# Low parts of attention keys padded with zeros to 128 rows, in a three-block kernel whose first loads and first block are also put in another order

## The chip, the cores and the metric

One Trainium2 chip, one core. The metric is device time in microseconds (us) of one execution of the whole program; a kernel's time is the median of several runs. The core has TensorE (PE in the profile, its weight loads apart as PEld), VectorE (DVE), ScalarE (ACT), GpSimd (POOL) and SyncE (SP), which here issues transfers alone. Each engine runs its own list of instructions in order; it waits where an instruction needs a result of another engine.

## The reference

Three blocks run one behind the other on one sequence `x` of 512 positions and 1024 features, all in fp32:

```
x = first_block(x, c, ctx, ...)    # three branches (below), gated and summed, then a SwiGLU FFN
x = second_block(x, ...)           # 2 layers: FFN, hybrid attention mixer, FFN
x = third_block(x, c_3, ...)       # RG-LRU and attention side by side

# first_block: h = modulate(rms_norm(x), shift, scale), and of p = h @ w_in
o  = gla_bidir(q, k, v, gates)     # gated linear attention, chunks of 64, both directions, 4 heads
y_a = (norm(o) * silu(r)) @ w_o_gla
hc = depthwise_conv(c1 * sigmoid(c2), 31 taps)
y_b = silu(layer_norm(hc)) @ w_o_conv
y_c = (su * spatial_mix(layer_norm(sv))) @ w_o_sgu
y  = (gate0 * y_a + gate1 * y_b + gate2 * y_c) @ w_out

# second_block, mixer: 8 heads of 64 with a forget gate, 4 differential heads with two maps of 64 each
s = q @ k.T * scale + cum_q - cum_k     # causal, softmax, @ v
a = softmax(s1) - lam * softmax(s2)     # differential heads
# third_block: 8 heads of 64, which for 512 positions is plain causal attention
```

The shift and scale of each block are `silu(c) @ w_ada + b_ada`.

## The kernel before

**Products.** Features lie on partitions: `x` is 8 tiles of 128x512. A large product of fp32 operands is made of three matmuls on operands split into a high and a low part of fp32r (`mm3`): high times high, high times low, low times high. Weights stream through SP in 542 chunks of 128x1024 into three buffers `wraw`; ACT casts a chunk's high part (`whi`), and DVE subtracts it to make the low part (`wlo`; of odd chunks POOL does, in the attention stretches). A chunk feeds 24 of these main matmuls, which is also what one output tile of 128x512 takes of 1024 inputs (a unit below).

**Order.** Everything else (norms, gated linear attention, convolution, attention) is background work, written as Python generators. Behind each `mm3` the builder steps them (`tick`), and a generator goes on when the builder's own clock (`Clock`, with a price per instruction from `cost_pe`, `cost_act`, `cost_dve`, `cost_pool`) says that its operands are there and that enough tiles are free (`sync`, `room`, `wait`). What comes out is a fixed list of instructions for each engine. Nothing is reordered on the chip, so the prices shape the order of every engine. There are 78 blocks of 128x512 for intermediates (`b`) and 8 PSUM banks (`bk`). Where blocks run out, the builder lets the main matmuls stand and steps the background alone (`need`, `idle`). Convolution taps are a filler that is put in between on DVE.

**Attention.** `stack` takes a tile that holds the transposed queries or keys of two heads (64 rows each) and makes operands of 128 rows. For queries, operand e holds the high part of head e in its own 64 rows and the low part in the other 64. For keys, operand e holds the high part in both halves, and one more tile holds the low parts of both heads. `attn_scores` makes a block of 128 queries against up to 512 keys of two matmuls: 128 rows (both parts of the queries with the keys' high part), and then 64 rows (queries' high part, keys' low part):

```python
k.nc.tensor.matmul(b[:, o:o + n], lhsT=q[e].r[:, c], rhs=kk[e].r[:, 0:n], start=True, stop=False)
k.nc.tensor.matmul(b[:, o:o + n], lhsT=q[e].r[rows, c], rhs=kk[2].r[rows, 0:n], start=False, stop=True)
```

Each head (or map) has four such pairs, with 256, 256, 384 and 512 keys. There are 16 heads or maps in each layer of block 2 (layer 0 at some 1650 to 1830 us of the trace, layer 1 at 2660 to 2850) and 8 in block 3 (some 3340 to 3450). That makes 160 pairs, and 20 stacks of keys.

**Block 1's middle.** `ORDER_1` sets the order of units: `r` (8 gate units of the linear attention), `g` (8 units of branch gates for each of three branches), `p` (8 output products for each branch), `a` (wait until the linear attention is done), `v` and `s` (third branch). Branch 0 is the linear attention, branch 1 the convolution. In the trace the first `r` begins at 271.4 us, the first product (of branch 1) at 506.2, the first of branch 0 at 564.2, and `v` at 622.2.

**Start.** `Ada1` makes shift and scale: SP loads pieces of `w_ada` in four parts of 8 tiles; part 0 is multiplied on PE (`rows`), the others on DVE (`step`, then `sums` on PE and `finish`). Part q serves tiles 2q and 2q+1 of the first loop. `warm` issues fp32 matmuls of a zeroed tile whose results nothing reads. `prepare` makes tile m of the normalized and modulated input.

Of the kernel before, what the change touches and what calls it, by code (L numbers as in the profile page):

```python
# [18 lines left out]
S = 512  # L19
SC = 256  # L20
KT = 8
# [156 lines left out]
def width(ap):  # L178
    n = 1
    for d in tuple(ap.shape)[1:]:  # L180
        n *= d
    return n
# [41 lines left out]
def cost_dve(op, out, a, kw):  # L224
    n = width(out)
    if op == "reciprocal":
        return 0.07 + 6.4e-3 * n
    if op in ("tensor_scalar", "memset"):
        return max(0.2, 0.1 + 0.7e-3 * n)
    return max(0.2, 0.08 + 1.05e-3 * n)  # L230


def cost_pool(op, out, a, kw):
    return 0.06 + (1.0e-3 if op == "memset" else 2.3e-3) * width(out)


class Engine:
# [532 lines left out]
def stack(k, t, keys):  # L770


    nc = k.nc
    yield from k.sync()
    yield from k.room(4)
    out = [k.rblk(), k.rblk()]
    low = k.rblk() if keys else None
    own = [slice(0, 64), slice(64, 128)]
    for e in range(2):
        nc.scalar.copy(out[e].r[own[e]], t.f[own[e]])  # L780
    if keys:
        for e in range(2):
            nc.scalar.copy(out[e].r[own[1 - e]], t.f[own[e]])
    yield from k.sync()
    for e in range(2):
        lo = (low.r if keys else out[e].r)[own[e] if keys else own[1 - e]]
        nc.gpsimd.tensor_sub(lo, t.f[own[e]], out[e].f[own[e]])
    k.free(t)
    if keys:
        out.append(low)  # L790
    return out


def attn_scores(k, q, kk, e, part):
    b = k.bank()
    rows = slice(64 * e, 64 * e + 64)
    for qb, o in part:
        n, c = max((qb + 1) * P, 256), slice(qb * P, qb * P + P)
        k.nc.tensor.matmul(b[:, o:o + n], lhsT=q[e].r[:, c], rhs=kk[e].r[:, 0:n], start=True, stop=False)
        k.nc.tensor.matmul(b[:, o:o + n], lhsT=q[e].r[rows, c], rhs=kk[2].r[rows, 0:n], start=False, stop=True)  # L800
    return b


# [222 lines left out]
class Diff:  # L1026
# [3 lines left out]
    o = None  # L1030
# [834 lines left out]
def some(kind, ms, b=None):  # L1865
    return [(kind, m, b) for m in ms]


def between(b, ahead):

    o = []
    for m in range(KT):
        o += some("p", [m], b)
        if m + ahead < KT:
# [1 line left out]
    return o  # L1876


ORDER_1 = (some("r", range(KT)) + some("g", range(6), 1) + some("g", range(6), 0) + between(1, 6) + some("a", [0])
           + between(0, 6) + some("v", range(2)) + some("s", range(KT)) + some("g", range(6), 2) + between(2, 6))  # L1880


def plan1():
# [75 lines left out]
class Ada1:  # L1959
# [20 lines left out]
    def rows(self, q):  # L1980

        k, nc = self.k, self.k.nc
        b, row = k.bank(), k.blk()
        for t in range(KT):
            nc.tensor.matmul(b[0:2], lhsT=self.sc[:, t, :], rhs=self.ws[q][t].f, start=t == 0, stop=t == KT - 1)
        nc.scalar.copy(row.f[0:2], b[0:2])
        k.unbank(b)
        b = k.bank()
        for i in range(4):
            nc.tensor.transpose(b[:, 2 * i:2 * i + 2], row.f[0:2, i * P:i * P + P], k.ident[0:2, 0:2])  # L1990
        for c in range(2):
            self.finish(q, c, b[:, c:8:2])
        k.unbank(b)
        k.free(row, self.ws.pop(q))

    def step(self, q, c, t, acc):
        ve, w, s = self.k.nc.vector, self.ws[q][t].f, self.sc[:, t, c:c + 1]
# [91 lines left out]
def gla_dir(k, st, h, s, res):  # L2089
    nc = k.nc  # L2090
    b = yield from k.gbank()
    c0 = s * 512 + h * P
    nc.tensor.matmul(b, lhsT=st["aup"][c0 // 512].r[0:96, c0 % 512:c0 % 512 + P], rhs=st["adn"].r[0:96],
                     start=True, stop=True)
# [43 lines left out]
                         start=True, stop=True)  # L2138
    pairs = lambda ap: ap.rearrange("p (b c t) -> p b c t", c=2, t=64)
    chunk = dec.rearrange("p (b c) -> p b c", c=2)  # L2140
    nc.gpsimd.tensor_mul(both, chunk[:, :, 0], chunk[:, :, 1])
    f, l = pairs(kd.f)[:, :, s], pairs(qe.f)[:, :, 1 - s]
    nc.gpsimd.tensor_mul(f, f, chunk[:, :, 1 - s:2 - s].to_broadcast([P, 4, 64]))
    nc.gpsimd.tensor_mul(l, l, chunk[:, :, s:s + 1].to_broadcast([P, 4, 64]))
# [284 lines left out]
def block1(k, x, nxt):  # L2429
    nc = k.nc  # L2430
    w = "w_in"
    st = dict(q={}, k={}, v={}, r={}, o={}, ck={}, cv={}, s0=[k.blk() for _ in range(4)], cdone=0, hdone=0,
              conv={}, hc={}, yb={}, z={}, sv={})
    for m in range(KT):
        x.append(k.blk())
        nc.sync.dma_start(x[m].f, k.a["x"][:, m, :])
    ada = Ada1(k)
    ada.load(0)
    k.w_start()
    ada.load(1)  # L2440
    warm(k, 7)
    k.clk.t = k.clk.c["dve"] = k.clk.c["act"] = 6.0
    acc = sumsq(k, [x[m].f for m in range(KT)], S, nc.vector)
    lt, ly = rms_cols(k, acc.f, S, EPS1)
    ada.rows(0)
    bcb = bc_rows(k, ly)
    hx = []

# [7 lines left out]
        k.free(x[m])  # L2456

    prepare(0)
    k.w_ensure(1)
    k.w_finish(1)  # L2460
    prepare(1)
    ada.load(2)
    cols = k.bank()
# [4 lines left out]
    for m in range(KT):  # L2468
        q = m // 2 + 1
        if m % 2 == 0 and q < 4:  # L2470
            k.fresh()
            for t in range(KT):
                ada.step(q, 0, t, gacc)
            summed = k.clk.t
        for n, c0 in enumerate(first_units()):
            k.main_mm3(fb[n], k.wnext(w, 0, m, c0), (hx[m][0].r, hx[m][1].r), m == 0, m == KT - 1)
            if m % 2 == 1 and n == 1 and q < 4:
                k.clk.t = summed
                ada.sums(cols[:, 4 * q:4 * q + 4], gacc)
                ada.finish(q, 0, cols[:, 4 * q:4 * q + 4])  # L2480
                for i in range(2):
                    prepare(m + 1 + i)
        if m == 0:
            ada.load(3)
        elif m == 2:
            for i in range(4):
                nc.scalar.dma_start(cq[i].f.rearrange("p (m t) -> p m t", t=SC), k.a["ctx"][:, 2 * i:2 * i + 2, :])
# [338 lines left out]
```

## Time and profile before

| | |
|---|---|
| median of 3 runs | 3515.91 us (3515.6 to 3515.91) |
| the profiled execution | 3511.07 us, span of its trace 3509.3 us |
| TensorE busy | 3405.3 us of the span |
| VectorE, ScalarE, GpSimd busy | 1911.7, 1351.7, 720.5 us |

A busy time is the time in which an engine has at least one instruction in work. The span runs from the first instruction to the last; the execution's own time lies 1.8 us above it. Matmuls overlap their neighbours, so the time that one takes of PE is the distance to the start of the next, not its recorded duration.

### The profile page before, as it was taken

What the parts mean: (1) busy time and instruction counts of PE and PEld (TensorE: products, weight loads), DVE (VectorE), ACT (ScalarE), POOL (GpSimd) and SP (SyncE); (2) the same over time, 40 slices, a digit from 0 to 9 for tenths busy, and PEclk for the clock granted to TensorE, in tenths of its full rate; (3) what the DMA queues carried; (4) which work ended last, traced back from release to release, by engine and by line L of the source; (5) the groups of instructions that cost most, each with busy time, mean ns of one, the idle gap of its engine ahead of it and who ended that gap; (6) DMA issues with size and microseconds to landing.
All of it is one profiled execution on the core that took longest, in us unless ns stands there. A gap on an engine that the chain in (4) does not pass through costs nothing.

```text
span 3509.3 us, 39437 instructions
## 1 busy us (share of the span) xinstructions
PE 3405.3 (97%) x15210; PEld 2763.3 (79%) x15210; DVE 1911.7 (54%) x3010; ACT 1351.7 (39%) x2176; POOL 720.5 (21%) x564
## 2 busy tenths in 40 slices
PE   7998889999999999999999999999999999999999
PEld 5886678887888888887778888888887778888777
DVE  5899865655333365433686443344335774433566
ACT  3324462223322332324764222233227653232474
POOL 0004231222000101103452110011016331111362
PEclk9998999999999999999999999999999999999999
DMA  6211114543322244232122222322332123222221
GB/s 209 93 56 55 48 49 149 181 156 102 102 98 99 99 159 164 97 117 98 55 68 80 99 97 96 96 96 97 107 108 72 60 68 108 96 96 96 72 79 55
DMA packets 110189, 344.99 MB, mean 98 GB/s; under 512 B 13425, under 2 KB 13681, under 8 KB 110001
## 3 DMA queue, kind: packets, MB, share of 16 engines
q1 hardware_dynamic: 84960, 296.78, 25.2%
q10 hardware_dynamic: 23760, 41.50, 3.7%
q0 software_dynamic: 1280, 4.20, 0.4%
q8 instruction: 119, 1.95, 0.2%
q14 instruction: 70, 0.57, 0.1%
HBM read 336.13 MB, written 6.29 MB: 98 GB/s over the span
## 4 chain that ended last, share of the span: by engine, by line
PE 52%; DVE 4%; ACT 2%; POOL 1%; issue 1%; DVEq 0%; POOLq 0%; ACTq 0%
PE bk L256 52%; DVE b L256 3%; ACT b L256 1%; DVE tinies L256 1%; POOL b L256 1%; POOL wlo L256 0%; DVE wlo L256 0%; ACT whi L256 0%; ACT L251 0%; ACT bk L256 0%; ACT tinies L256 0%; DVE small L256 0%; DVEq L256 0%; POOLq L256 0%; ACTq L256 0%
## 5 line engine op out<-in xcount | busy, mean ns | idle before, releaser
L256 PE MATMUL bk<-b,whi 128*128 128x512 f32 (+1 forms) x8048 | 2514.7, 394 | 6.8 <-ACT whi L256 3.4
L256 PEld LDWEIGHTS bk<-b,whi 128*128 128x128 f32 x8048 | 1506.7, 190 | 323.3 <-issue 9.6
L256 PE MATMUL bk<-b,wlo 128*128 128x512 f32 (+1 forms) x4024 | 1575.4, 391 | 6.7 <-DVE wlo L256 5.9
L256 POOL TENSOR_TENSOR b<-b,b 128x512 f32<-128x512 f32 (+2 forms) x381 | 528.4, 1395 | 2391.1 <-DVE b L256 1189.4
L256 DVE TENSOR_TENSOR wlo<-wraw,whi 128x1024 fp32r<-128x1024 f32 x495 | 643.8, 1303 | 528.8 <-ACT whi L256 528.5
L256 PEld LDWEIGHTS bk<-b,wlo 128*128 128x128 f32 x4024 | 762.2, 189 | 170.1 <-DVE wlo L256 8.8
L256 ACT CAST whi<-wraw 128x1024 fp32r<-128x1024 f32 x542 | 568.0, 1049 | 739.8 <-PE bk L256 442.8
L256 ACT CAST b<-b 128x512 fp32r<-128x512 f32 (+3 forms) x286 | 176.0, 618 | 523.9 <-POOL b L256 369.9
L256 DVE TENSOR_TENSOR b<-bk,b 128x512 f32<-128x512 f32 (+6 forms) x324 | 208.1, 659 | 253.7 <-PE bk L256 212.9
L256 DVE TENSOR_TENSOR b<-b,b 128x512 fp32r<-128x512 f32 (+3 forms) x250 | 184.7, 745 | 251.0 <-ACT b L256 248.9
L256 PE MATMUL bk<-b,b 128*128 128x128 f32 (+9 forms) x1056 | 250.4, 354 | 33.2 <-POOL b L256 20.4
L256 ACT ACTIVATE b<-b 128x512 f32<-128x512 f32 (+1 forms) x259 | 153.4, 608 | 308.7 <-DVE b L256 273.1
L256 PEld LDWEIGHTS bk<-b,b 128*128 128x128 f32 (+3 forms) x1056 | 174.1, 193 | 109.9 <-issue 36.0
L256 PE MATMUL bk<-whi,b 128*128 128x512 f32 x768 | 248.4, 397 | 4.0 <-ACT b L256 2.2
L256 DVE SCALAR_TENSOR_TENSOR b<-b,pvt,b 128x392 f32<-128x392 f32 (+7 forms) x296 | 229.0, 778 | 33.3 <-ACT b L256 26.4
L256 PEld LDWEIGHTS bk<-whi,b 128*128 128x128 f32 x768 | 145.6, 190 | 36.6 <-DVE b L256 3.0
L256 DVE SCALAR_TENSOR_TENSOR b<-b,small,b 128x512 f32<-128x512 f32 (+1 forms) x178 | 148.0, 833 | 20.8 <-ACT b L256 15.5
L256 POOL TENSOR_TENSOR wlo<-wraw,whi 128x1024 fp32r<-128x1024 f32 x47 | 116.0, 2467 | 202.3 <-ACT whi L256 175.7
L256 PE MATMUL bk<-wlo,b 128*128 128x512 f32 x384 | 150.8, 393 | 0.0
L256 PE MATMUL bk<-cst,b 128*128 128x128 f32 (+1 forms) x776 | 111.5, 271 | 36.3 <-DVE b L256 25.3
L256 PEld LDWEIGHTS bk<-cst,b 128*128 128x128 f32 x776 | 98.9, 168 | 60.4 <-DVE b L256 31.8
L256 ACT ACTIVATE b<-bk 128x512 f32<-128x512 f32 (+2 forms) x170 | 97.2, 572 | 111.6 <-PE bk L256 109.9
(93 smaller groups left out, 1233.9 us busy)
## 6 DMA issues: line engine op xcount, KB each, us to landing
wraw<-in_wst SPq DMA_DIRECT2D x542, 512.0 KB, 3.3
b<-in_ada1r ACTq DMA_DIRECT2D x64, 256.0 KB, 4.4
b<-in_ada ACTq DMA_DIRECT2D x48, 256.0 KB, 4.1
b<-in_ada SPq DMA_DIRECT2D x32, 256.0 KB, 5.5
xpark<-b ACTq DMA_DIRECT2D x16, 256.0 KB, 2.0
b<-xpark POOLq DMA_DIRECT2D x16, 256.0 KB, 5.2
b<-in_x SPq DMA_DIRECT2D x8, 256.0 KB, 5.2
b<-in_x ACTq DMA_DIRECT2D x8, 256.0 KB, 4.5
```

What stands on the lines that cost most here:

```text
L256: return f(*a, **kw)
```

## The change

Five edits, in one diff:

1. The keys' low parts get a tile per head, whose other 64 rows ScalarE fills with zeros (a copy of a zero of the mask, broadcast). The second matmul of a pair runs over 128 rows. A stack of keys takes five blocks in place of four.
2. The builder's prices change: DVE scans and convolution taps, and POOL operations.
3. `ORDER_1`: all 16 gate units of branches 0 and 1 ahead of the products; branch 0's products ahead of branch 1's.
4. A small product of the linear attention (`both`, 128x4, eight times) goes from POOL to DVE.
5. At the start, part 0 of `w_ada` is loaded ahead of `x`, and part 1 behind the first weight chunk; `rows` runs ahead of the sum of squares; `warm` is split in two; `sums` stands two units later in the first loop.

```diff
+    if op == "tensor_tensor_scan":
+        return 0.03 + 2.2e-3 * n
+    if op == "scalar_tensor_tensor" and n > 300 and len(tuple(out.shape)) == 3:
+        return 0.2 + 1.1e-3 * n
...
-    return 0.06 + (1.0e-3 if op == "memset" else 2.3e-3) * width(out)
+    return 0.06 + 1.0e-3 * width(out) if op == "memset" else max(0.5, 0.1 + 2.7e-3 * width(out))
...
-    yield from k.room(4)
+    yield from k.room(5 if keys else 4)
     out = [k.rblk(), k.rblk()]
-    low = k.rblk() if keys else None
+    lows = [k.rblk(), k.rblk()] if keys else out
...
             nc.scalar.copy(out[e].r[own[1 - e]], t.f[own[e]])
+            nc.scalar.copy(lows[e].r[own[1 - e]], k.c("mask")[own[1 - e], 0:1].to_broadcast([64, S]))
...
-        k.nc.tensor.matmul(b[:, o:o + n], lhsT=q[e].r[rows, c], rhs=kk[2].r[rows, 0:n], start=False, stop=True)
+        k.nc.tensor.matmul(b[:, o:o + n], lhsT=q[e].r[:, c], rhs=kk[2 + e].r[:, 0:n], start=False, stop=True)
...
-ORDER_1 = (some("r", range(KT)) + some("g", range(6), 1) + some("g", range(6), 0) + between(1, 6) + some("a", [0])
-           + between(0, 6) + some("v", range(2)) + some("s", range(KT)) + some("g", range(6), 2) + between(2, 6))
+ORDER_1 = (some("r", range(KT)) + some("g", range(KT), 0) + some("g", range(KT), 1) + some("a", [0]) + between(0, KT)
+           + between(1, KT) + some("v", range(2)) + some("s", range(KT)) + some("g", range(6), 2) + between(2, 6))
...
-    nc.gpsimd.tensor_mul(both, chunk[:, :, 0], chunk[:, :, 1])
+    nc.vector.tensor_mul(both, chunk[:, :, 0], chunk[:, :, 1])
...
+    ada = Ada1(k)
+    ada.load(0)
     for m in range(KT):
         x.append(k.blk())
         nc.sync.dma_start(x[m].f, k.a["x"][:, m, :])
-    ada = Ada1(k)
-    ada.load(0)
+    k.w_start(1)
+    ada.load(1)
     k.w_start()
-    ada.load(1)
-    warm(k, 7)
+    row = ada.rows(0)
+    warm(k, 3)
...
-    ada.rows(0)
+    ada.turn(0, row)
+    k.w_ensure(0)
+    k.w_finish(0)
+    warm(k, 3)
     bcb = bc_rows(k, ly)
...
-    k.w_ensure(1)
-    k.w_finish(1)
...
-            if m % 2 == 1 and n == 1 and q < 4:
+            if m % 2 == 1 and n == 3 and q < 4:
```

`turn` is the second half of what was `rows`: the copy of the row, its transposes and `finish`. Since prices shape the order, edits 1 to 3 move background work all over the program. Three places show it.

**Attention of layer 0, on PE.** Matmuls with `whi` or `wlo` are main ones; rows that share their bank and their last operand by twos are pairs of scores. Before, some 50 rows ahead of the end of the score work, pairs stand between mains:

```order
L256 MATMUL bk_69<-b_751_9837,whi_83 128x512
L256 MATMUL bk_69<-b_752_9838,whi_83 128x512
L256 MATMUL bk_69<-b_751_9837,wlo_86 128x512
L256 MATMUL bk_72<-b_867_11321,b_864_11267 128x512
L256 MATMUL bk_72<-b_868_11322,b_864_11267 128x512
L256 MATMUL bk_71<-b_867_11321,b_864_11267 128x384
L256 MATMUL bk_71<-b_868_11322,b_864_11267 128x384
L256 MATMUL bk_69<-b_754_9921,whi_83 128x512
L256 MATMUL bk_69<-b_755_9922,whi_83 128x512
L256 MATMUL bk_69<-b_754_9921,wlo_86 128x512
L256 MATMUL bk_68<-b_867_11321,b_864_11267 128x256
```

With the change, in the same place (the 98 matmuls of PE's list around it have no main among them; the longest such run before has 56):

```order
L260 MATMUL bk_70<-b_872_11264,b_859_11157 128x384
L260 MATMUL bk_70<-b_874_11266,b_859_11157 128x384
L260 MATMUL bk_72<-b_872_11264,b_859_11157 128x256
L260 MATMUL bk_72<-b_874_11266,b_859_11157 128x256
L260 MATMUL bk_72<-b_872_11264,b_859_11157 128x256
L260 MATMUL bk_72<-b_874_11266,b_859_11157 128x256
L260 MATMUL bk_68<-b_873_11265,b_860_11158 128x512
L260 MATMUL bk_68<-b_875_11267,b_860_11158 128x512
L260 MATMUL bk_73<-b_873_11265,b_860_11158 128x384
L260 MATMUL bk_73<-b_875_11267,b_860_11158 128x384
L260 MATMUL bk_66<-b_898_11512,b_827_10871 128x512
L260 MATMUL bk_66<-b_899_11513,b_827_10871 128x512
```

The pairs moved out from between the mains and stand together, with products of other heads (`bk_66<-b_898,b_827` and on) among them. The shape printed is that of the output, so the second row of a pair reads alike in both.

**Block 1's middle, on PE.** The row `bk<-cst,b 128x1 x4` sums the convolution's squares for its variance. Before, it stands in the second gate unit of branch 0, 15 units behind the first `r`:

```order
L256 MATMUL bk_70<-b_64_317,whi_83 128x512
L256 MATMUL bk_70<-b_65_318,whi_83 128x512
L256 MATMUL bk_70<-b_64_317,wlo_86 128x512
L256 MATMUL bk_66<-b_222_2847,b_224_2849 64x64 x4
L256 MATMUL bk_68<-b_228_2873,b_229_2874 128x128 x4
L256 MATMUL bk_71<-cst,b_111_1107 128x1 x4
L256 MATMUL bk_70<-b_66_323,whi_83 128x512
L256 MATMUL bk_70<-b_67_324,whi_83 128x512
L256 MATMUL bk_70<-b_66_323,wlo_86 128x512
```

With the change it stands in the first product of branch 0, 24 units behind the first `r`:

```order
L260 MATMUL bk_73<-b_205_2669,whi_83 128x512
L260 MATMUL bk_73<-b_206_2670,whi_83 128x512
L260 MATMUL bk_73<-b_205_2669,wlo_86 128x512
L260 MATMUL bk_73<-b_220_2822,whi_83 128x512
L260 MATMUL bk_73<-b_221_2823,whi_83 128x512
L260 MATMUL bk_73<-b_220_2822,wlo_86 128x512
L260 MATMUL bk_68<-cst,b_112_1143 128x1 x4
L260 MATMUL bk_73<-b_222_2841,whi_83 128x512
L260 MATMUL bk_73<-b_223_2842,whi_83 128x512
L260 MATMUL bk_73<-b_222_2841,wlo_86 128x512
```

The convolution's sum moved back by nine units, and the first branch product came forward to it.

**The start, on DVE.** `b_40` here is the low part of tile 0, `bk_70` or `bk_71` the broadcast norm, and `b_39` ahead of a `MEMSET` the zeroed tile of the second `warm`. Before:

```order
L256 SCALAR_TENSOR_TENSOR small<-small,pvt 128x2
L256 TENSOR_TENSOR small<-bk_69,pvt 128x4
L256 SCALAR_TENSOR_TENSOR small<-small,pvt 128x2
L256 TENSOR_TENSOR b_5_95<-b_5_95,bk_70 128x512
L256 TENSOR_TENSOR b_40_222<-b_5_95,b_39_221 128x512
L256 TENSOR_TENSOR wlo_86<-wraw_80,whi_83 128x1024
L256 TENSOR_TENSOR wlo_87<-wraw_81,whi_84 128x1024
L256 TENSOR_TENSOR b_6_97<-b_6_97,bk_70 128x512
L256 TENSOR_TENSOR b_42_234<-b_6_97,b_41_233 128x512
L256 TENSOR_SCALAR b_51_254<-b_21_134,small 128x512
```

With the change:

```order
L260 SCALAR_TENSOR_TENSOR small<-small,pvt 128x2
L260 TENSOR_TENSOR small<-bk_69,pvt 128x4
L260 SCALAR_TENSOR_TENSOR small<-small,pvt 128x2
L260 TENSOR_TENSOR wlo_86<-wraw_80,whi_83 128x1024
L260 MEMSET b_39_215 128x512
L260 TENSOR_TENSOR b_13_115<-b_13_115,bk_71 128x512
L260 TENSOR_TENSOR b_41_226<-b_13_115,b_40_225 128x512
L260 TENSOR_TENSOR b_14_117<-b_14_117,bk_71 128x512
L260 TENSOR_TENSOR b_43_232<-b_14_117,b_42_231 128x512
L260 TENSOR_SCALAR b_52_252<-b_21_132,small 128x512
```

The first weight's low part and the zeroed tile moved ahead of the broadcast norm's first use, and the second weight's low part (`wlo_87`) moved behind the eight steps of part 1, of which the first is the last row here.

## Rows read from the trace of the kernel before

**Rows 1.** The page: the span, and busy time of each engine.

```profile
span 3509.3 us, 39437 instructions
PE 3405.3 (97%) x15210; PEld 2763.3 (79%) x15210; DVE 1911.7 (54%) x3010; ACT 1351.7 (39%) x2176; POOL 720.5 (21%) x564
```

**Rows 2.** Stretches: length, busy time of each engine, granted clock, share of DMA, GB/s.

```profile
30.00:83.00 53.00, 43.37 (x169) 34.51 (x168) 36.80 (x54) 20.54 (x25) 0.00 (x0) 0.85 0.52 176
83.00:271.00 188.00, 187.01 (x894) 156.87 (x893) 168.30 (x260) 50.81 (x75) 0.00 (x0) 1.00 0.24 78
267.70:533.90 266.20, 226.23 (x1042) 182.37 (x1041) 218.77 (x311) 143.15 (x276) 94.95 (x84) 0.90 0.16 52
271.00:622.00 351.00, 309.79 (x1412) 251.06 (x1412) 263.52 (x356) 165.14 (x302) 105.77 (x91) 0.93 0.24 79
1650.00:1830.00 180.00, 173.16 (x750) 126.77 (x749) 133.20 (x355) 126.88 (x297) 93.66 (x73) 0.94 0.17 55
2660.00:2850.00 190.00, 184.28 (x799) 135.83 (x799) 137.63 (x375) 130.16 (x305) 102.93 (x82) 0.96 0.20 66
1795.96:1806.61 10.65, 9.48 (x60) 7.78 (x59) 9.78 (x31) 8.87 (x20) 3.06 (x4) 1.00 0.01 2
```

**Rows 3.** Waits of PE in 271 to 506 us: us in total, times, longest us.

```profile
PE bk L256 <- POOL b L256: 19.3, 10, 3.3
PE bk L256 <- DVE b L256: 16.9, 4, 7.9
PE bk L256 <- ACT b L256: 2.5, 2, 2.2
```

**Rows 4.** Timeline of PE in layer 0: start, duration, operation; scores among main matmuls.

```profile
1677.91 3.15 PE L256 MATMUL bk<-b,b 128*128 128x512 f32 x8
1680.99 0.73 PE L256 MATMUL bk<-b,whi 128*128 128x512 f32 x2
...
1742.21 0.61 PE L256 MATMUL bk<-b,whi 128*128 128x512 f32 x2
...
1744.93 2.46 PE L256 MATMUL bk<-b,b 128*128 128x256 f32 x8
1747.32 0.73 PE L256 MATMUL bk<-b,whi 128*128 128x512 f32 x2
```

**Rows 5.** Timeline of PE in layer 0: products of probabilities and values, transposes.

```profile
1795.95 0.98 PE L256 MATMUL bk<-b,b 128*128 128x512 f32 x4
1796.77 1.25 PE L256 MATMUL bk<-cst,b 128*128 128x128 f32 x10
1797.78 0.72 PE L256 MATMUL bk<-b,b 128*128 128x256 f32 x4
1798.34 0.93 PE L256 MATMUL bk<-cst,b 128*128 128x128 f32 x7
```

**Rows 6.** Groups by shape, of DVE, ACT and POOL: busy us, mean ns.

```profile
L256 DVE TENSOR_TENSOR tinies<-tinies 128x4 f32<-128x4 f32 x76 | 15.4, 202 | 2.6
...
L256 ACT CAST b<-b 64x512 fp32r<-64x512 f32 x120 | 74.0, 616 | 4.1 <-POOL b L256 1.9 <-DVE b L256 0.2
...
L256 POOL TENSOR_TENSOR b<-b,b 128x512 f32<-128x512 f32 x285 | 401.3, 1418 | 2056.3 <-ACT b L256 1058.4 <-DVE b L256 903.4 <-issue 51.2
L256 POOL TENSOR_TENSOR tinies<-tinies 128x4 f32<-128x4 f32 x8 | 5.6, 705 | 0.0
```

**Rows 7.** Timeline of PE: the convolution's variance; the linear attention's last transposes.

```profile
454.57 1.87 PE L256 MATMUL bk<-cst,b 128*128 128x1 f32 x8 [7.92 <-DVE b L256]
...
519.57 0.60 PE L256 MATMUL bk<-cst,b 128*128 128x128 f32 x4
```

**Rows 8.** Timeline of PE at the start, with the idle time ahead.

```profile
24.70 1.16 PE L256 MATMUL bk<-cst,tinies 128*128 128x128 f32 x8
29.26 1.22 PE L256 MATMUL bk<-b,whi 128*128 128x512 f32 x2 [3.41 <-ACT whi L256]
...
40.59 1.87 PE L256 MATMUL bk<-cst,b 128*128 128x1 f32 x8 [3.84 <-DVE b L256]
```

More of the change, by code (lines that the diff above doesn't have):

```diff
@@ L783, in stack @@
             nc.scalar.copy(out[e].r[own[1 - e]], t.f[own[e]])
+            nc.scalar.copy(lows[e].r[own[1 - e]], k.c("mask")[own[1 - e], 0:1].to_broadcast([64, S]))
     yield from k.sync()
     for e in range(2):
-        lo = (low.r if keys else out[e].r)[own[e] if keys else own[1 - e]]
-        nc.gpsimd.tensor_sub(lo, t.f[own[e]], out[e].f[own[e]])
+        nc.gpsimd.tensor_sub(lows[e].r[own[e] if keys else own[1 - e]], t.f[own[e]], out[e].f[own[e]])
     k.free(t)
-    if keys:
-        out.append(low)
-    return out
+    return out + lows if keys else out
 def attn_scores(k, q, kk, e, part):
     b = k.bank()
-    rows = slice(64 * e, 64 * e + 64)
     for qb, o in part:
@@ L1982, in rows, with turn @@
         k, nc = self.k, self.k.nc
-        b, row = k.bank(), k.blk()
+        b = k.bank()
         for t in range(KT):
             nc.tensor.matmul(b[0:2], lhsT=self.sc[:, t, :], rhs=self.ws[q][t].f, start=t == 0, stop=t == KT - 1)
+        k.free(self.ws.pop(q))
+        return b
+    def turn(self, q, b):
+        k, nc = self.k, self.k.nc
+        row = k.blk()
         nc.scalar.copy(row.f[0:2], b[0:2])
@@ L1993, in rows @@
         k.unbank(b)
-        k.free(row, self.ws.pop(q))
+        k.free(row)
     def step(self, q, c, t, acc):
```

## The prediction

> **What bounds the kernel now.** First the busy times of the page: TensorE is at work for 3405.3 of 3509.3 us, and no other engine passes 1911.7 [rows 1]. So time can be won where PE does work that it need not do, or where it stands. I read the stretches next [rows 2]. In 83 to 271 us PE is busy for 187.01 of 188. In the middle of block 1 it is not: from 271 to 622 us, 351 us pass with 309.79 busy at a granted clock of 0.93 of full. These 351 us hold 40 units of 24 main matmuls. A main matmul takes 0.227 us where nothing else stands between (12 of them from 1742.21 to 1744.93 us [rows 4]), so 40 units are 218 us; the other matmuls there, each at its full-speed distance to the next, sum to 55 by my count over the trace. Some 75 to 80 us are lost, nearly all ahead of the first product at 506 us. The waits of PE there name POOL 19.3 us, DVE 16.9 and ACT 2.5 [rows 3], the longest one 7.9 us, for the convolution's variance [rows 7]. The rest is the lower clock (a granted 0.93 is 1.2 GHz in place of 2.4 for a seventh of the stretch; it fell behind such stalls), and small gaps between matmuls.
>
> The mixers' stretches lose less (PE busy 173.16 of 180 and 184.28 of 190 us [rows 2]), but part of that busy time is dear. Eight matmuls of four score pairs (512, 512, 384, 384 columns, twice) take from 1677.91 to 1680.99 us, and eight of 256 columns from 1744.93 to 1747.32 [rows 4]. Four products with 128 rows and 512, 512, 384, 384 columns take from 1795.95 to 1796.77 us, and four with 256 from 1797.78 to 1798.34 [rows 5]. So the same columns cost 3.08 us as two sets of pairs and 1.64 as two sets of products; for 256 columns it is 2.39 against 1.12. All ran at the full clock.
>
> **Edit 1, the rows.** What differs is the second matmul of each pair: 64 rows between neighbours of 128. The difference is 1.44 us for four pairs in the one case and 1.27 in the other, 0.36 and 0.32 us a pair; against the main pitch of 0.227 us (half of it for 256 columns) it is up to 0.39. With 160 pairs that makes 51 to 62 us. I take 0.36: 58 us, of which 23 lie in each layer of block 2 (64 pairs) and 12 in block 3 (32). The columns stay the same, and the 128-row products in [rows 5] show that rows themselves cost nothing.
>
> The trace thus shows some 0.18 us at each change between 128 and 64 rows, twice a pair. The Trainium skill, "TensorE: Matmul & The Clock Gate", section "Back-to-back issue gap", would let the spacing depend on the columns alone, some 216 ns for 512 at the full clock; by it the pairs cost nothing extra and the edit brings 0. The same skill's "TensorEngine Tiling (Array Packing)", section "Key Properties", has an exception: a change of the tiling mode makes the engine drain. It gives no price. The trace agrees with the exception.
>
> What edit 1 adds: 40 copies of 64x512 on ACT, 0.616 us each [rows 6], 16 of them (10 us) in each layer, where ACT is busy for 126.88 of 180 us [rows 2]. They lie beside PE's work and cost nothing, unless ACT is behind: at most 25 us in all.
>
> **Where that gain goes.** A stack takes one block more, and the new order shows what follows: in layer 0 the builder runs out of blocks, lets the mains stand and gathers attention work (98 matmuls without a main; before, 56). I counted what DVE's list holds between the low parts of weights, each row priced at the median of its shape in the trace of before. In layer 0, from chunk 265 to 268, DVE has 77 us of work and PE 50 (96 mains, 22 us, and 221 others). DVE's busy time in 1650 to 1830 us, 133.2, is 5% above such a sum for that stretch, so 80 us: a surplus of 30. Before, the worst place (chunks 267 and 268) has 33 us of DVE against 24 of PE, and its 56 matmuls took 10.65 us with DVE busy for 9.78 and PE for 9.48 [rows 2]: a surplus of 9 cost little over 1, since weights are prepared up to three chunks ahead. So 8 are absorbed and 22 stay. **Layer 0: −23 + 22 = −1 us.** In layer 1 (chunks 429 to 434) it is 79 against 56, 15 stay: **−23 + 15 = −8.** In block 3 (chunks 533 to 538) DVE's 51 face PE's 52: **−12, less 3 for copies and the later end of its work, −9.** Bounds: nothing absorbed and DVE 19% dearer (its recorded durations, overlaps counted double, against the medians): 41 and 34 us, layers +18 and +11. All absorbed: −23 each.
>
> **Edits 2 to 4, block 1's middle.** The change puts 24 units ahead of the first product, not 20, and moves the convolution's variance back by nine units, so the 7.9 us wait [rows 7] and most of those for POOL should go. POOL's 128x512 operations take 1.418 us [rows 6] where the old price said 1.24 and the new says 1.48, so the order waits for them later. `both` on DVE adds 8 × 0.20 us there and takes 8 × 0.71 from POOL [rows 6].
>
> But DVE then sets the pace. From chunk 33 (the first `r`) to 59, the low parts' times are 267.7 and 533.9 us: 266.2 us, with DVE busy for 218.77 [rows 2]. By medians, DVE's list holds 188 us there, so it takes 16% more than these, with POOL at work beside it. The new list holds 198, that is 229 at the same surcharge; PE needs 26 × 5.45 + 55 = 197. Were DVE never idle, chunk 59 would come at 497 us, 37 us sooner. It is at work for 92% of the time where it was the limit (9.78 of 10.65 [rows 2]), and for 90% in 83 to 271; I take 93%, 246 us: 20 sooner. Behind it, chunks 59 to 63 hold 25 us of DVE (27 with surcharge) where before 20.5 passed: 6 back. **Block 1: −14.** Bounds: 0 (DVE idle as much as before), and −60 (DVE catches up behind the branches, PE alone is the limit).
>
> **Edit 5, the start.** Before, PE ends the broadcast norm some 25.9 us in, and the first main starts at 29.26, having waited 3.41 for the weight's high part; the first `sums` wait 3.84, until 40.59 [rows 8]. With the change the weight is ready early, but the second `warm` needs a tile that DVE zeroes behind `wlo_86`, and the norm comes some 2.3 us later by the same durations. `wlo_87` stands behind the eight steps, so unit 2 waits for it, at 41 to 42 us. The `sums` are no longer in that way, yet the later tiles follow them, about 2 us later than now. The last `sums` come with less behind them. **+1**, bounds −3 and +5; 30 to 83 us has PE busy for 43.37 of 53 [rows 2], so the loss there is no more than it was.
>
> **Sum.** −1 − 8 − 9 − 14 + 1 = −31 us. The profiled execution took 3511 us, so 3480; the median of the runs lies 5 above it: 3485. Nearer to the middle of the bounds, since three of them reach further down than up, I say **3480**.
>
> **Rivals.**
> - *PE stays the limit everywhere.* DVE's lumps are absorbed and block 1 recovers 60: −58 − 60 + 1, 3399. For it: DVE is busy for 54% of the span [rows 1], and its lists even out over longer stretches. Against it: DVE at 92% where scores bunch. One of the two halves alone gives 3430 (block 1) or 3455 (attention).
> - *Attention gains nothing, block 1 its 14.* Bunches cost what the rows save: some 3503. It holds if layers 0 and 1 stand for 50 us together; I count 37.
> - *Slower: blocks.* Mains stand while DVE and ACT work through bunches: at the upper bounds, 41 + 34 us of standing and 4 in block 3 are 79 against 58 saved; with block 1 at 0, 3537. It decides from 58 + 14 = 72 us of standing.
> - *The rows don't matter.* If the 0.36 us belong to scores and not to the change of rows, edit 1 saves 0 and its bunches cost 37: 3511 − 14 + 1 + 37, slower, 3540 with the median's 5. Against it stand the products, alike in all but rows [rows 4, 5].
> - *The linear attention is late.* Its products now come first, and its last transposes stand one unit ahead of them. From the first `r` to those transposes 248 us pass now (to 519.57 [rows 7]); were it so again, `v` would come at about 520 + 5 + 16 × 5.45 = 612, still not later than 622. So this takes the gain of block 1, no more.
>
> **How the numbers follow.** My forecast (3460 to 3500) has 0.45; PE the limit everywhere, or nearly (under 3430), 0.10, one half of it (3430 to 3460) 0.20; attention gaining nothing (3500 to 3515) 0.15; blocks 0.06 and rows 0.04, of which 0.07 lie above 3523. The range reaches from 3430 to 3513 and leaves out about 0.2. A measurement of this kernel can tell 0.2%, 7 us. Faster by more than that (under 3509): 0.86; within it 0.07; slower 0.07.
>
> **What would show it.** Scores: no 64-row form is left, and eight matmuls of pairs take some 1.6 us where they took 3.08. Bunches: PE stands for 15 to 25 us in each mixer of block 2, waiting for DVE or ACT, at a lower clock. Block 1: `v` begins at about 608 us, DVE is busy for over 90% up to the first product, and PE waits for `wlo`. Start: the first main at about 30 us. I am wrong if DVE is idle while PE stands, or if PE stands for under 10 us in layer 0.

## The result, and the profile after

The changed kernel takes 3474.66 us (median of 4 runs, 3473.58 to 3474.80) where the kernel before takes 3515.88: a ratio of 0.9882, with a 95% interval of 0.9865 to 0.9899. I had said 3480, within 3430 to 3513. Its profiled execution has a span of 3472.8 us, 36.5 below that of before; the median fell by 41, since the profiled execution of before lay 5 us below its own median.

The page of the changed kernel, with the lines that answer to [rows 1]:

```profile
span 3472.8 us, 39481 instructions
PE 3344.5 (96%) x15208; PEld 2755.5 (79%) x15208; DVE 1910.2 (55%) x3017; ACT 1376.7 (40%) x2221; POOL 719.3 (21%) x556
```

PE is busy for 61 us less, but the span is only 36 shorter: PE stands for 24 us more than before. The stretches tell where. Below are the same pieces of work in both kernels, cut at the same main matmuls: layer 0, layer 1, block 3 and block 1's middle (first `r` to `v`). Columns are those of [rows 2]. Before:

```profile
1658.00:1886.00 228.00, 221.16 (x969) 164.70 (x968) 167.15 (x432) 146.88 (x338) 110.53 (x91) 0.96 0.19 62
2666.60:2906.80 240.20, 232.48 (x1034) 174.74 (x1032) 179.49 (x453) 151.03 (x345) 113.06 (x93) 0.96 0.20 66
3358.10:3505.10 147.00, 141.13 (x648) 109.05 (x647) 96.26 (x223) 92.31 (x176) 59.15 (x49) 0.98 0.18 63
271.40:622.20 350.80, 309.59 (x1410) 250.88 (x1409) 263.15 (x355) 164.98 (x303) 105.77 (x91) 0.93 0.24 79
```

With the change:

```profile
1633.60:1849.70 216.10, 196.10 (x969) 161.06 (x968) 164.21 (x431) 155.16 (x355) 111.75 (x90) 0.96 0.19 66
2631.50:2870.30 238.80, 213.24 (x1034) 175.32 (x1033) 175.60 (x452) 161.57 (x362) 115.03 (x93) 0.94 0.20 66
3321.60:3468.70 147.10, 133.91 (x649) 111.72 (x647) 100.89 (x224) 97.03 (x185) 58.86 (x48) 0.94 0.18 61
272.40:599.40 327.00, 298.32 (x1418) 242.96 (x1417) 274.58 (x384) 165.94 (x305) 103.69 (x83) 0.98 0.27 88
```

Layer 0 takes 216.1 us in place of 228.0, layer 1 238.8 in place of 240.2, block 3 147.1 in place of 147.0, block 1's middle 327.0 in place of 350.8. PE's idle time (length less busy) goes from 6.8 to 20.0, from 7.7 to 25.6 and from 5.9 to 13.2 us in the three attention stretches, and from 41.2 to 28.7 in block 1. So in attention PE does less and stands more; in block 1 it stands less, and its clock rises from 0.93 to 0.98.

The rows themselves did what [rows 4, 5] promised. The timeline of PE, layer 0 of the changed kernel, start and duration:

```profile
1670.02 1.07 PE L260 MATMUL bk<-b,b 128*128 128x512 f32 x4
1670.93 0.39 PE L260 MATMUL bk<-whi,b 128*128 128x512 f32 x1
...
1693.97 1.11 PE L260 MATMUL bk<-b,b 128*128 128x256 f32 x8
1694.92 0.63 PE L260 MATMUL bk<-b,whi 128*128 128x512 f32 x2
```

Eight matmuls of 256 columns now take 0.95 us (1693.97 to 1694.92); before they took 2.39 [rows 4]. Four of 512 columns take 0.91.

The waits of PE in the changed kernel (us in total, times, longest) show new names. First layer 1 (2631.5 to 2870.3 us), then block 3 (3321.6 to 3468.7), and then block 1's middle up to the first product:

```profile
PE bk L260 <- DVE b L260: 13.5, 8, 4.4
PE bk L260 <- DVE tinies L260: 6.0, 4, 3.7
PE bk L260 <- DVE wlo L260: 6.0, 3, 2.1
...
PE bk L260 <- ACT b L260: 10.4, 4, 4.8
PE bk L260 <- POOL wlo L260: 2.1, 1, 2.1
...
PE bk L260 <- POOL b L260: 12.3, 7, 3.4
PE bk L260 <- ACT b L260: 8.8, 4, 7.4
...
PE bk L260 <- DVE wlo L260: 1.9, 1, 1.9
```

And single waits, in the brackets at the end of a row of the timeline:

```profile
454.03 7.60 PE L260 MATMUL bk<-b,b 128*128 128x256 f32 x24 [7.41 <-ACT b L260]
...
3392.53 2.28 PE L260 MATMUL bk<-b,b 128*128 128x512 f32 x4 [4.79 <-ACT b L260]
...
3453.24 0.52 PE L260 MATMUL bk<-b,whi 128*128 128x512 f32 x1 [3.38 <-ACT b L260]
```

The first row is the wait in block 1 that took the place of [rows 7]; the others, all for ACT, are in block 3, the last one for the operands of the last product.

What the other engines do while PE stands differs too. By my count over the trace, DVE is at work in 19.3 of the 20.0 us in layer 0 and in 24.5 of the 25.6 in layer 1, but in only 3.4 of the 13.2 in block 3, where ACT is at work in 10.7.

### The profile page after: what moved, and what is told of

It is laid out like the page before. It is cut to its first block, busy times and chain, and to the rows that moved or that the text cites. A ratio compares the mean times of both kernels' runs of the same rounds, so it can differ in the third digit from the quotient of the medians.

```text
span 3472.8 us, 39481 instructions
## 1 busy us (share of the span) xinstructions
PE 3344.5 (96%) x15208; PEld 2755.5 (79%) x15208; DVE 1910.2 (55%) x3017; ACT 1376.7 (40%) x2221; POOL 719.3 (21%) x556
## 4 chain that ended last, share of the span: by engine, by line
PE 49%; DVE 5%; ACT 4%; issue 1%; POOL 1%; POOLq 0%; DVEq 0%; ACTq 0%
PE bk L260 49%; ACT b L260 3%; DVE b L260 3%; DVE tinies L260 1%; POOL b L260 0%; ACT whi L260 0%; DVE wlo L260 0%; ACT L255 0%; POOL wlo L260 0%; ACT bk L260 0%; POOLq L2831 0%; DVEq L260 0%; ACT tinies L260 0%; DVE small L260 0%; POOLq L260 0%
## 5 line engine op out<-in xcount | busy, mean ns | idle before, releaser
L260 PE MATMUL bk<-b,wlo 128*128 128x512 f32 (+1 forms) x4024 | 1571.5, 391 | 16.8 <-DVE wlo L260 14.6
L260 DVE SCALAR_TENSOR_TENSOR b<-b,pvt,b 128x392 f32<-128x392 f32 (+7 forms) x296 | 236.8, 804 | 33.0 <-ACT b L260 26.4
L260 PE MATMUL bk<-b,b 128*128 128x256 f32 (+6 forms) x1056 | 202.9, 334 | 39.5 <-ACT b L260 19.1
L260 PEld LDWEIGHTS bk<-b,b 128*128 128x128 f32 (+2 forms) x1056 | 168.4, 199 | 69.9 <-POOL b L260 20.6
L260 PEld LDWEIGHTS bk<-cst,b 128*128 128x128 f32 x776 | 99.1, 168 | 60.2 <-DVE b L260 36.5
```

The source lines that it names most:

```text
L260: return f(*a, **kw)
```

## The experiments

All times are medians; the kernel before, run beside them, took 3517 to 3519. The table gives, for each kernel, the change against before of the time between the same two main matmuls, in us. Each row comes from one trace. Up to the first `r` the lists of e1, e3, e5, e7 and e8 are those of before, and yet that column spreads from -2.1 to +0.4 for them; so differences of 1 to 3 us say nothing.

| kernel | time | up to the first `r` | block 1's middle | layer 0 | layer 1 | block 3 |
|---|---|---|---|---|---|---|
| changed | 3474.7 | +1.0 | -23.8 | -12.0 | -1.4 | 0.0 |
| e1 padding only | 3489.6 | 0 | 0 | -10.9 | -9.1 | -1.1 |
| e2 all but padding | 3493.6 | +0.9 | -23.2 | +1.3 | +4.4 | +2.8 |
| e3 shared low tile | 3475.4 | +0.4 | +1.6 | -12.7 | -18.7 | -7.1 |
| e4 shared, all else | 3461.7 | +0.8 | -24.0 | -9.2 | -9.8 | -4.1 |
| e5 e3, short scaling | 3465.0 | -1.9 | +1.5 | -15.2 | -19.5 | -9.7 |
| e6 changed, short taps | 3461.2 | +1.0 | -37.1 | -12.0 | -1.5 | 0.0 |
| e7 order of units only | 3515.5 | +0.4 | 0 | +1.3 | -0.1 | 0.0 |
| e8 e3 and order of units | 3474.0 | -2.1 | -1.3 | -12.2 | -17.7 | -7.0 |
| e9 prices only | 3523.3 | -3.0 | +6.8 | +2.3 | +5.8 | +2.6 |
| e10 e4, higher prices | 3508.5 | +3.3 | -11.5 | +4.3 | +3.7 | +0.6 |
| e11 e4, later signals | 3476.1 | +1.8 | -13.2 | -21.2 | +6.2 | -3.9 |
| e12 e4, short runs | 3444.0 | +0.4 | -24.0 | -18.2 | -19.3 | -6.7 |

**e1 and e2: the two halves apart.** e1 takes only edit 1 (`stack` and `attn_scores` of the diff), e2 all the rest.

> Edit 1 alone on the kernel before (zero-padded low parts, a fifth block per stack of keys); prices, block 1 and start as before. Theory T (the change of rows was worth 0.36 to 0.40 us a pair, some 62 us; the fifth block makes the builder bunch attention work, and PE stands for most of that again): the bunch of layer 0 is 108 matmuls long, so it gains as much as the three attention stretches gained in the changed kernel, 13 us, give or take 10: 3493 to 3513. Rival R2 (the bunches, and with them the standing, come from the new prices, not from the block): the whole of the rows arrives, 3450 to 3465. Rival R1 (DVE and ACT cannot follow a PE that is faster in attention, however the work is laid out): 3495 to 3510, like T.

> The changed kernel without edit 1: scores and stacks of keys as before, new prices, new order of block 1, new start. T: block 1 and the start give what they gave in the changed kernel (v sooner by some 23 us), attention stays within 8 us of the kernel before: 3485 to 3501. R2: the new prices bunch attention work by themselves, and with the changes of rows still paid the attention stretches lose 20 us or more: over 3505.

e1: 3489.56 us, ratio 0.9922 (0.9907 to 0.9937). e2: 3493.64, 0.9932 (0.9917 to 0.9946). R2 falls: the prices are not what eats the rows' gain, for e1 has the old ones and gains 21 us in attention, not 50 or 60. e1 came out better than T's range. The halves alone win 27 and 24 us and together 41: in layer 1 padding alone wins 9, the rest alone loses 4, and both together win 1.4.

**e3 and e4: 128 rows without zeros.** The second matmul runs over the whole shared tile of low parts; stacks stay as they were.

```diff
-        k.nc.tensor.matmul(b[:, o:o + n], lhsT=q[e].r[rows, c], rhs=kk[2].r[rows, 0:n], start=False, stop=True)
+        k.nc.tensor.matmul(b[:, o:o + n], lhsT=q[e].r[:, c], rhs=kk[2].r[:, 0:n], start=False, stop=True)
```

> The kernel before with one edit: the second matmul of a pair runs over all 128 rows of the shared tile of low parts, no zeros, no fifth block. It adds the product of the queries' low part with the other head's low keys, a term as small as the low-by-low product that the kernel leaves out anyway. The order of every engine is that of the kernel before. T: the rows' gain arrives without bunches, less a little standing: 3455 to 3475. R1: DVE and ACT cannot follow, so PE stands for what it saves: 3495 to 3510.

> As e3, with the new prices, the new order of block 1 and the new start (the changed kernel without zeros and fifth block). T: the gains add, 3516 - 23 - 50: 3430 to 3452, below the changed kernel. R1: 3475 to 3485, no better than the changed kernel.

e3: 3475.35, ratio 0.9880 (0.9865 to 0.9895): one line gives as much as the whole change. e4: 3461.74, 0.9841 (0.9824 to 0.9857), 13 below the changed kernel, though above the 3430 to 3452 of T. Both theories get a part. e3 wins 38.5 us in attention where the rows are worth 59 (below), so 20 of them do not arrive although no instruction changed its place in its engine's list; and the zero tiles with their copies and their fifth block cost 17 beside that (e1 wins 21 with the same order of units and the same prices; no run parts the copies from the block). The stretches of e3, in the order layer 0, layer 1, block 3:

```profile
1661.50:1876.90 215.40, 193.93 (x969) 159.11 (x968) 164.78 (x432) 146.74 (x338) 111.39 (x91) 0.98 0.19 66
2657.50:2878.90 221.40, 204.20 (x1033) 168.60 (x1032) 185.28 (x453) 151.38 (x345) 114.21 (x93) 0.98 0.21 71
3329.10:3469.00 139.90, 129.83 (x648) 108.81 (x647) 98.38 (x223) 91.96 (x176) 60.13 (x49) 0.96 0.19 66
```

PE's idle time is 21.5, 17.2 and 10.1 us, where it was 6.8, 7.7 and 5.9. That is 28 us more, of which the better clock of the two layers gives some 8 back.

**e5 and e6: less work for DVE, same order.** An operation is charged at its full price to the builder and issued over a part of its columns. e5 does it to the scaling of probabilities, on e3; e6 to every other convolution tap, on the changed kernel.

```diff
-            ve.tensor_scalar(v, v, self.sm.f[:, 16 + qb:17 + qb], None, op0=ALU.mult)
+            ve._clk.add("dve", cost_dve("tensor_scalar", v, (), {}))
+            ve._e.tensor_scalar(v[:, 0:8], v[:, 0:8], self.sm.f[:, 16 + qb:17 + qb], None, op0=ALU.mult)
```

> e3 with one DVE operation of the attention made short: the scaling of the probabilities (96 tiles of 128 to 512 columns in block 2's forget-gate heads and block 3) runs over 8 columns only, so most probabilities stay unscaled; the order of every engine is that of e3. It takes some 15 us of DVE's time out of each attention stretch. Theory D (DVE's amount of work sets the pace where PE stands, some 14 us more than before in each layer): each layer of block 2 gains 6 to 14 us and block 3 up to 5 on e3's 3475: 3443 to 3462. Rival C (PE waits for a chain that goes from engine to engine, whose length hardly depends on how full DVE is): 3467 to 3475.

> The changed kernel with every other convolution tap on DVE run over one row of 64 positions in place of eight, so the convolution is incomplete; the order of every engine stays that of the changed kernel. Some 70 taps behind the first r are shortened, by 0.55 us each: 39 us less of DVE's work in block 1's middle. Theory D (DVE sets the pace there): v begins 20 to 35 us sooner, 3440 to 3455. Rival C (POOL and ACT chains of the linear attention set it): less than 7 us sooner, 3468 or more.

e5: 3464.96, ratio 0.9849 (0.9831 to 0.9867), 10 below e3. In the profiled executions it is 7 below, of which 2.3 lie ahead of the first `r`; the three stretches win 2.5, 0.8 and 2.6 on e3. e6: 3461.19, 0.9839 (0.9823 to 0.9855), 13.5 below the changed kernel, all of it in block 1's middle. Both lie between D and C, and the premise was off: a shortened operation still took time. Over 8 columns the scaling took 414 ns in the mean (e5), and a tap over an eighth of its columns 300 to 610 ns in block 1's middle (the last section says why these means are so high). So DVE's busy time fell by 15 us in e5 (1917.3 to 1902.0 over the span), not by 15 in each stretch. The stretches of e5, layer 0, layer 1 and block 3, to be set beside those of e3:

```profile
1659.30:1872.20 212.90, 195.55 (x970) 161.79 (x969) 159.82 (x433) 146.44 (x338) 109.86 (x91) 0.96 0.20 67
2652.80:2873.40 220.60, 205.41 (x1033) 169.97 (x1032) 179.56 (x453) 151.47 (x345) 113.90 (x93) 0.98 0.21 72
3324.90:3462.30 137.40, 128.86 (x649) 108.47 (x648) 94.39 (x223) 91.95 (x176) 60.06 (x48) 0.98 0.19 68
```

DVE is busy for 5.0, 5.7 and 4.0 us less. In block 1's middle, e6 takes 22 us, not 39:

```profile
272.40:586.10 313.70, 296.79 (x1418) 243.29 (x1417) 253.10 (x382) 166.02 (x305) 100.34 (x83) 0.98 0.27 92
```

(It is 22 us more in the changed kernel, above.) Per us of DVE's time taken away, PE came 0.6 us sooner in block 1, and 0.4 in attention. These runs do not decide between D and C: an operation made shorter also shortens each chain that it stands in, and e5's gains in a stretch are no larger than the spread from trace to trace. How much of the standing is DVE's amount of work, and how much a chain, is not shown.

**e7 to e9: what helps in block 1.** e7 has `ORDER_1` of the change alone; e8 has it with `both` on DVE, on e3; e9 has the new prices alone.

> The new ORDER_1 alone on the kernel before; prices, start, both and scores as before. Theory O (what helps in block 1 is the place of the convolution's statistics and products, behind four more gate units): 16 to 28 us faster, 3488 to 3500. Rival P (the new prices for POOL and DVE take the waits away, and the order of units alone does little): within 7 us of 3516.

> e3 with the new ORDER_1 and the move of both to DVE, but with the old prices and the old start. If O holds, e3's gain and that of the order add: 3475 - 22, 3446 to 3460, no slower than e4 (3462), since the old prices cost attention less. If P holds: 3470 to 3476.

> The new prices alone on the kernel before; order of units, start, both and scores as before. The order of units alone (e7) gave nothing. Theory P (the prices empty PE's waits in block 1): v some 20 us sooner, 3492 to 3502, attention within 5 us of before. Rival PO (prices and order of units only help together): less than 8 us faster, 3508 or more.

e7: 3515.46, ratio 0.9992 (0.9980 to 1.0003). e8: 3473.97, as e3. e9: 3523.33, 1.0010 (1.0000 to 1.0020). So neither the order of units nor the prices help block 1 (0 and +6.8 us); together, in e2, they give -23. Rival PO holds, with one reservation: e2 also has the new start and `both` on DVE, and no run has the prices and the order of units alone. With e7 the convolution's statistics stand where they stood before, 11 and 15 units behind the first `r`, and PE waits for them as before. With e9 the prices put them 20 units behind it, and there, in the old order of units, the convolution's products begin, which need them. The timeline of PE in e9, start, duration and the wait ahead:

```profile
497.33 1.87 PE L260 MATMUL bk<-cst,b 128*128 128x1 f32 x8 [1.82 <-DVE b L260]
...
508.60 0.65 PE L260 MATMUL bk<-b,whi 128*128 128x512 f32 x1 [3.79 <-ACT b L260]
511.91 0.80 PE L260 MATMUL bk<-b,whi 128*128 128x512 f32 x1 [2.67 <-DVE b L260]
```

The variance (497.33) comes 11 us ahead of the first product (508.60), and that waits 3.79 us for ACT and then 2.67 for DVE. The new order of units puts branch 0's eight products ahead of them. That this is why the two edits need each other is read from lists and waits; no run moved the products alone.

**e10 and e11: is the builder's clock too fast?** e10 raises prices on e4, e11 the time for a signal (`LAT`).

```diff
-    return 0.08 + 0.9e-3 * width(out)
+    return 0.16 + 0.9e-3 * width(out)
...
-    if op in ("tensor_scalar", "memset"):
+    if op == "memset":
         return max(0.2, 0.1 + 0.7e-3 * n)
-    return max(0.2, 0.08 + 1.05e-3 * n)
+    if op == "tensor_scalar":
+        return max(0.2, 0.2 + 0.8e-3 * n)
+    return max(0.2, 0.12 + 1.12e-3 * n)
```

> e4 with ACT's and DVE's prices raised to what the trace shows (ACT 512 columns 0.62 us, was 0.54; DVE tensor_tensor 0.69, was 0.62; tensor_scalar 0.61, was 0.46), so the order takes results later. Theory L (with 128 rows everywhere PE runs as fast as the builder's clock, and chains that the clock prices too low come late; the slow pairs had hidden that): attention's three stretches gain 15 to 30 us on e4, 3432 to 3447. Rival B (what counts is where blocks run out and mains stand; this order has runs of 57, 48 and 46 matmuls without a main): within 10 us of e4, 3452 to 3472.

> e4 with the builder's allowance for a signal from one engine to another raised from 0.1 to 0.2 us, prices as in the changed kernel. Theory L: chains of five to ten signals a step come less late, 5 to 20 us faster than e4, 3442 to 3457. Rival B (longest run without a main 58 here, 61 in e4): within 5 us of e4.

e10: 3508.47, ratio 0.9968 (0.9956 to 0.9980); e11: 3476.12, 0.9869 (0.9852 to 0.9887). Theory L falls: prices nearer to the trace cost 47 us on e4, of which 32 lie in the attention stretches, and later signals cost 14. Of these 14, though, 11 lie in block 1's middle; in attention e11 wins 12 in layer 0 and loses 16 in layer 1 against e4. Rival B, which expected no more than 10, falls in its numbers too. One and the same price list thus helps one layer and hurts the other. One thing that differs between the layers is where the builder lets mains stand. I counted, in each kernel's list of PE, the runs of over 25 attention matmuls without a main one, and set their sum in layer 1 beside PE's idle time there and the stretch's length:

| | e3 | e12 | e4 | e1 | changed | e10 | e11 |
|---|---|---|---|---|---|---|---|
| matmuls in such runs | 0 | 0 | 39 | 44 | 51 | 91 | 86 |
| PE idle, us | 17.2 | 16.8 | 19.7 | 21.9 | 25.6 | 27.2 | 28.8 |
| of it in such runs, us | 0.0 | 0.0 | 6.1 | 3.0 | 3.9 | 8.0 | 5.9 |
| length, us | 221.4 | 220.9 | 230.4 | 231.0 | 238.8 | 243.9 | 246.4 |

e3 and e12 have the same lists in this layer, so they count as one. Idle time grows with the runs, and the length grows about twice as much, since the clock falls with it (0.98 granted in e3, 0.94 in the changed kernel, 0.92 in e11). But the runs are not the place where PE stands: they hold 8 us of it at most, and 14 to 23 us lie elsewhere. The changed kernel's run of 51, in the columns of the stretches:

```profile
2765.10:2778.30 13.20, 9.32 (x51) 7.79 (x51) 12.16 (x50) 11.74 (x30) 6.86 (x10) 0.85 0.00 0
```

PE is idle for 3.9 us in it. Of the other 21.7 us in that layer, 15.7 come with shorter groups of background matmuls and 6.0 between mains. So the count goes along with the standing in layer 1 and does not explain most of it. In layer 0 it fails even as a sign: e12, with no such run, is idle for 17.0 us, and e11, with one run of 36, for 14.1; e3, e4, e1 and the changed kernel, with 57, 61, 108 and 143, for 20 to 22; e10, with 113, for 28.2.

**e12: an order chosen by that count.** New prices in block 1 alone, old ones behind it, and `LAT` 0.13 in layer 0, on e4:

```diff
+def phase(k, new, lat):
+    NEW[0], k.clk.LAT = new, lat
...
     for l in range(2):
+        phase(k, *((False, 0.13), (False, 0.1))[l])
...
+        phase(k, *(False, 0.1))
         block3(k, x, n3, o["out"])
```

> e4 (shared low tile, new order of block 1, new start) with the new prices in block 1 alone; behind it the old prices, and in layer 0 an allowance of 0.13 us for a signal. That was chosen because its lists have no long runs of attention matmuls without a main one: at most 20 in layer 0 (e4: 61, e3: 57), at most 19 in layer 1 (e4: 39), at most 38 in block 3. Theory B (standing follows those runs): layer 0 gains 18 to 24 us on the kernel before (e4 9, e3 13), layer 1 16 to 20, block 3 some 7; with 23 from block 1 it comes to 3438 to 3452, the fastest so far. Rival N (what an order brings in attention follows from no such count): layer 0 within 5 us of e3 and e4, 3452 to 3465.

3443.95 us, ratio 0.9795 (0.9782 to 0.9808), the fastest of all: 31 us below the changed kernel. The stretches of e12, layer 0, layer 1, block 3 and block 1's middle:

```profile
1632.90:1842.80 209.90, 192.85 (x970) 157.83 (x969) 169.00 (x430) 146.59 (x341) 110.63 (x91) 0.98 0.19 68
2623.40:2844.30 220.90, 204.08 (x1034) 168.80 (x1032) 183.44 (x453) 151.64 (x345) 114.92 (x93) 0.98 0.21 71
3295.70:3436.00 140.30, 130.46 (x649) 109.62 (x647) 98.12 (x223) 92.08 (x176) 61.10 (x48) 0.96 0.19 66
271.80:598.60 326.80, 299.50 (x1418) 243.56 (x1417) 274.83 (x384) 165.97 (x306) 103.48 (x83) 0.97 0.26 88
```

Layer 0 wins 18.2 us, layer 1 19.3 and block 3 6.7, within theory B's numbers (18 to 24, 16 to 20, 7). PE is idle for 17.0, 16.8 and 9.8 us there, the granted clock is 0.98, 0.98 and 0.96. But this tests B in layer 0 alone: in layer 1 and block 3 every engine's list is that of e3, by a comparison of the two traces, and e3 had won 18.7 and 7.1 there. In layer 0 e12 lies 9 us ahead of e4 and 5.5 ahead of e3, where rival N allowed 5, and the total lies below N's 3452; so N is the weaker of the two, but by one layer of one order. Of the 31 us below the changed kernel, e3 alone has 25.

## Why the prediction was right, and where it was not

**The rows: right.** I had 58 us (23, 23, 12). Taking from each stretch its idle time and what matmuls took over their full-clock distance while the clock was low (9.0, 7.6 and 2.2 us before; 6.6, 13.4 and 6.3 after), what is left falls from 212.3 to 189.5, from 224.9 to 199.8 and from 138.9 to 127.5: 22.8, 25.1 and 11.4, in all 59. The same count on e3, whose lists are those of before, gives 59 too. The upper bound of 62 does not come out of the rows: against the main pitch a pair costs 0.37 us, not 0.39, which makes 60. The rival on this (the cost belongs to scores, not to the change of rows) falls by the 0.95 us for eight matmuls of 256 columns. The Trainium skill's exception ("TensorEngine Tiling (Array Packing)", "Key Properties": a change of the tiling mode drains the engine) agrees: 1.44 us less for eight changes, 0.18 each.

**Where the gain went: right in kind, wrong in place.** That PE would stand and give back most of it was the step that decided the result. I had 22, 15 and 0 us of standing against 23, 23 and 12. Measured, idle time and low clock together rose by 10.8 in layer 0 (13.2 idle, the clock a little better), 23.7 in layer 1 (17.9 and 5.8) and 11.4 in block 3 (7.3 and 4.1). The sum, 46 against 37 with copies aside, is near; the parts are not.

The step that failed is the surplus of DVE's work, counted where scores bunch: it made layer 0 the worst and block 3 free. In the two layers its kind fits, since DVE is at work in 43.8 of the 45.6 us in which PE stands, and my sign of being wrong (DVE idle while PE stands) does not show there. Its size and its place do not fit: in layer 0 the runs of 45 and 98 matmuls hold 12.3 us of idle time (the run of before holds 1.2), where I had 22 more, and in layer 1 the run of 51 holds 3.9 of 25.6. In block 3 the sign does show: DVE is at work in 3.4 of the 13.2 us, the waits name ACT for 10.4, and the term that I had put at 0 is 11.4.

Bunches are also not needed for standing. In e3 20 of the 59 us do not arrive though every list is that of before, and in layer 1 it has no run of over 25 and still 17.2 us idle. What sets this standing stays open: DVE's amount of work, chains from engine to engine, and POOL's hold on DVE (last section) were not parted. Why the fifth block lengthens runs was only read from the lists; no run gave the change more blocks.

**Block 1: sign right, 10 us too small.** I had -14; it is -23.8. The low part of chunk 59 came at 513.2 us by the trace, 20.7 sooner, and I had 20; that agreement is luck. I had 246 us from the low part of chunk 33 to that of 59. It took 256, with DVE at work for 225 (I had 229), which is 88% of the time and not 93:

```profile
257.20:513.20 256.00, 227.84 (x1113) 185.11 (x1111) 225.06 (x327) 131.12 (x261) 91.97 (x76) 0.97 0.17 57
```

So half of the 20.7 us is that chunk 33 itself was ready 10.5 us sooner, which was not in my sum. I also took back 6 behind chunk 59, and nothing was given back. PE waited 1.9 us for `wlo`, less than for POOL (12.3) or ACT (8.8), so by its waits the low parts did not set the pace, though DVE was at work in 25.6 of the 27.2 us in which PE stood up to the first product. And I left the clock out of the sum: of the 23.8, 12.5 are idle time and the rest is nearly all clock, which rose to 0.98. Nor did I see that the prices or the order of units alone bring nothing (e7, e9).

**The sum: near by luck.** For layer 0, layer 1, block 3, block 1 and the start I had -1, -8, -9, -14 and +1, in all -31. The table has -12.0, -1.4, 0.0, -23.8 and +1.0, in all -36. Four of the five terms missed by 7 to 11 us, two in each direction.

**The start: right.** +1.0 at the first `r`. The timeline of PE in the changed kernel:

```profile
23.36 4.44 PE L260 MATMUL bk<-b 128*128 128x512 f32 x6 [4.32 <-DVE b L260]
...
30.32 0.49 PE L260 MATMUL bk<-b,whi 128*128 128x512 f32 x1 [1.63 <-ACT b L260]
...
41.96 0.79 PE L260 MATMUL bk<-b,wlo 128*128 128x512 f32 x1 [4.11 <-DVE wlo L260]
```

The second `warm` waits 4.32 us for its zeroed tile, the first main starts at 30.32, and unit 2 waits for `wlo_87` until 41.96; I had about 30, and 41 to 42.

**The other signs, and the rivals.** `v` begins at 599.4, not at 608, and DVE was at work for 88% of the time up to the first product, not over 90. PE stands for 20.0 and 25.6 us in the layers, about the 15 to 25 that I had; its clock is lower than before in layer 1 alone. The rivals: PE the limit everywhere (3399) did not come about; e12 is nearest to it, with 44 of 59 us in attention. Slower by blocks did not come about either: idle and low clock rose by 46 in attention, short of the 72 from which it decides.

## What to carry to other kernels

A matmul with fewer rows between others of full height cost 0.18 us at each change here; before filling up with zeros, look for an operand already at hand whose other half adds only a term of the size that is left out anyway (e3: one line, no copies, no tile). A saving on the busiest engine arrives only as far as the others keep up with it: the rows were worth 59 us, and with every list unchanged 38.5 arrived. Before laying standing to one cause, see in the trace where the idle time lies; here the long runs without mains looked like the cause and held 3.9 of 25.6 us in layer 1. And test two orders together before throwing either away: in block 1 neither the prices nor the order of units gave anything alone.

## What the runs showed of the hardware

A short DVE operation that runs beside one of POOL can last until POOL's ends. Rows of DVE and POOL in e5:

```profile
1776.31 0.23 DVE L963 TENSOR_SCALAR b<-b,tinies 128x8 f32<-128x8 f32 x1
1778.71 0.62 DVE L963 TENSOR_SCALAR b<-b,tinies 128x8 f32<-128x8 f32 x1
...
1778.03 1.27 POOL L256 TENSOR_TENSOR b<-b,cst 128x512 f32<-128x512 f32 x1 [8.56 <-ACT b L256]
```

The same scaling over 8 columns takes 0.23 us with POOL idle and 0.62 beside POOL, where both end at 1779.3. Of the 96 in e5, 79 took 218 to 345 ns and 17 took 0.6 to 2.2 us, which lifts the mean to 414; the median is 231 (281 to 490 over the 128 to 512 columns of e3). Each of the 17 ran beside a POOL operation and ended 26 to 33 ns behind its end. In e6 it is the same with 17 of the 112 taps over 50 to 62 columns: they took 0.5 to 1.4 us and ended 66 to 81 ns behind a POOL operation, and none of the other 95, all under 0.4 us, had one beside it.

In layer 1, moreover, the clock doubled the price of standing: from e3 to e11, 11.6 us more of idle time made the stretch 25.0 us longer, with the same products and scores. By my count 11 of the other 13 us are what matmuls took longer while the clock was at 1.2 GHz (0.98 granted in e3, 0.92 in e11).
